# Issuing 16 small row-to-column DMAs from GpSimd's queue instead of ScalarE's

## The chip, the cores and the metric

The kernel runs on one core of a Trainium2 chip. The metric is the time of one execution on the device in microseconds; the time before is the median of three runs. Traces come from one more execution under the hardware profiler. Engines are written as in the profile: PE is TensorE (PEld its weight loads), DVE VectorE, ACT ScalarE, POOL GpSimd, SP the sync engine, whose queue issues most DMAs; a q behind a name (SPq, ACTq) is that engine's instruction queue, waiting or issuing.

## The reference

A decoder of two layers on 256 tokens of width 1024, conditioned by a vector c. From silu(c) a matrix product gives each layer six vectors (shift, scale and gate of the mixer and of the experts) and two more for the shared keys and values. Layer 0 is a short gated convolution, layer 1 a causal differential attention with 8 heads; each is followed by 16 routed experts (one group of four, two experts in it). Cut to what matters:

```python
def reference(x, c, mod_w, mod_b, ...):
    c_act = jax.nn.silu(c)
    for l in range(DEPTH):
        m = c_act @ mod_w[l] + mod_b[l]
        sh_a, sc_a, gt_a, sh_f, sc_f, gt_f = jnp.split(m, 6, axis=-1)
        if l == N_A:
            k1, k2, v = shared_kv(x, c, kv_mod_w, kv_mod_b, kv_norm_g, kv_w)
        h = modulate(rmsnorm(x, norm_mix_g[l]), sh_a, sc_a)     # h * (1 + scale) + shift
        y = short_conv_mixer(h, ...) if l < N_A else diff_attention(h, k1, k2, v, ...)
        x = x + gt_a[:, None, :] * y
        h = modulate(rmsnorm(x, norm_ffn_g[l]), sh_f, sc_f)
        y = hier_moe(h, ...)
        x = x + gt_f[:, None, :] * y
    return rmsnorm(x, final_norm_g)
```

## The kernel before

All weights, some 295 MB in float32, pass once through the core. They are cut into tiles of 1 MB (128 partitions of 8 KB) in one long list, `stream`, in the order of use; `upto` issues them one after the other on SP's queue (line 162) into a pool of 15 buffers, `w`. SP thus runs ahead of the computation until it must wait for a buffer to be read out.

The projections (conv in and out, key/value, query, output) split each weight into a high part `whi` (a copy to float32r, line 58, on ACT, a few of the output weights on GpSimd, line 198) and a low part `wlo` (a subtraction on VectorE, line 61), some three steps ahead of TensorE (lines 228 and 233). The experts use the weights as they are: line 599 multiplies by w1 and w3, line 627 by w2, 12 tiles for a pair of experts, eight pairs in each layer.

The conditioning vectors are made beside this by the class `Vecs`: eight `step`s, each with one 1 MB tile, put into the projection loops by `tick`, accumulate 2048 values in one PSUM bank (line 323). At the eighth step ACT copies them to SBUF as `vrow` (line 328): four rows of 512. Some of the vectors are wanted as columns, value d on partition d / 8, since modulation works by partition there. For these, `column` issues two DMAs of 2 KB each, 64 partitions of 8 values, from one row of `vrow` into a tile `pcs` (line 336). This happens in six of the seven vector groups: 2, 2, 4, 4, 2 and 2 DMAs. The columns are read by VectorE in `shift_scale` (lines 365 and 367). Each engine runs its instructions in the order in which the program is written (the schedule is manual); so in ACT's queue the DMAs stand right behind `vrow` and ahead of the next weight parts and PSUM copies.

How a DMA tells that it has landed is not written in the kernel but laid out by the tile framework: DMAs issued by SP and ACT share eight completion counters (DMAHW0 to DMAHW7 in the built program), which they take in turn, and those issued by GpSimd take eight others (DMASW0 to DMASW7). An issue waits until everything that was put on its counter before has landed.

Of the kernel before, what the change touches and what calls it, by code (L numbers as in the profile page):

```python
# [33 lines left out]
def tile_yoco_trunk(ctx: ExitStack, tc: tile.TileContext,  # L34
# [5 lines left out]
    PE, V, A, G = nc.tensor, nc.vector, nc.scalar, nc.gpsimd  # L40
# [266 lines left out]
    class Vecs:  # L307
# [24 lines left out]
        def column(self, v):  # L332

            c = self.cols[v] = sm.tile([128, K], F32, name="pcs", bufs=4)
            for h in range(2):
                A.dma_start(c[64 * h:64 * h + 64], self.rows[32 * (2 * v + h):32 * (2 * v + h) + 1])

        def columns(self):

# [616 lines left out]
    for j in range(4):  # L956
# [18 lines left out]
        for u in range(2):  # L975
            if j < 2:
                h = 4 * j + 2 * u
# [228 lines left out]
```

## Time and profile before

| | |
|---|---|
| median of three runs | 818.91 us (818.17 to 819.31) |
| the profiled execution | 820.68 us, its span 818.9 us |
| TensorE busy | 748.8 us, 91% of the span |
| ScalarE, VectorE, GpSimd busy | 221.2, 274.1 and 78.9 us |
| mean granted TensorE clock | 0.984 |
| DMA | 296.76 MB, mean 362 GB/s, up to 423 GB/s in a slice |
| column DMAs on ACT's queue | 16 of 2 KB |

The span is from the first to the last instruction; the 1.8 us around it belong to the execution's time. Stages by time: vectors of the first layer and conv to 164 us, routing and experts of layer 0 to 412, keys, values and queries to 500, attention and output to 577, routing and experts of layer 1 to the end. In timelines the number in brackets is the time that the engine stood idle before the row and the work that ended it.

### The profile page before, as it was taken

The numbers are of one execution on the slowest core, as the hardware profiler recorded it, in microseconds if no ns is written. First come the engines' busy times: TensorE is split into PE (matmuls) and PEld (weight loads), VectorE is DVE, ScalarE is ACT, GpSimd is POOL, SyncE is SP. The second block draws the span as 40 slices with busy tenths as digits, with TensorE's granted clock in tenths as the row PEclk, the third lists the DMA queues.
The fourth block names the chain that finished last, engine by engine and source line by source line (L and its number), as shares of the span: only waits on it lengthen the run. The fifth ranks groups of instructions, "written<-read, shape, count | busy, mean of one in ns | idle before, by whom it ended". The sixth has DMA issues, their size and how long they took to land. (4 is left out here: it accounts for less than half of the span.)

```text
span 818.9 us, 10570 instructions
## 1 busy us (share of the span) xinstructions
PE 748.8 (91%) x4130; PEld 414.1 (51%) x4139; DVE 274.1 (33%) x586; ACT 221.2 (27%) x484; POOL 78.9 (10%) x97
## 2 busy tenths in 40 slices
PE   2899999999998799998879999998899999999985
PEld 2488786654343443332368577766543335434331
DVE  0337346462102312211272353674622124112113
ACT  3343233333010120010152454763321112111102
POOL 1000000100111011001030000332001110111001
PEclk9999999999999999999999999998999999999998
DMA  9999895839999999999999999685089999999993
GB/s 370 403 402 406 335 405 222 347 128 423 421 421 421 422 419 420 422 421 421 412 412 403 404 396 344 218 290 177 1 327 401 421 421 421 421 421 421 422 396 138
DMA packets 57734, 296.76 MB, mean 362 GB/s; under 512 B 6403, under 2 KB 6692, under 8 KB 26958
## 3 DMA queue, kind: packets, MB, share of 16 engines
q1 hardware_dynamic: 56326, 295.90, 90.0%
q8 instruction: 34, 0.56, 0.3%
q10 hardware_dynamic: 1352, 0.12, 0.1%
q14 instruction: 22, 0.18, 0.1%
HBM read 294.92 MB, written 1.05 MB: 361 GB/s over the span
## 5 line engine op out<-in xcount | busy, mean ns | idle before, releaser
L599 PE MATMUL pw<-w,xg 128*64 128x512 f32 x1024 | 230.1, 594 | 11.5 <-DMA w<-in_exp_w_dram 10.0
L599 PEld LDWEIGHTS pw<-w,xg 128*64 128x64 f32 x1024 | 76.8, 137 | 153.3 <-issue 127.6
L627 PE MATMUL py<-w,hidT 128*64 128x512 f32 x512 | 119.0, 597 | 7.0 <-DMA w<-in_exp_w_dram 4.8
L61 DVE TENSOR_TENSOR wlo<-w,whi 128x512 fp32r<-128x512 f32 x128 | 84.6, 694 | 114.8 <-ACT whi L58 103.0
L58 ACT ACTIVATE whi<-w 128x512 fp32r<-128x512 f32 x122 | 71.3, 625 | 53.0 <-PE pci L228 26.1
L608 DVE TENSOR_TENSOR silu<-silu,pw 128x512 f32<-128x512 f32 x16 | 11.0, 688 | 215.3 <-PE pw L599 215.3
L627 PEld LDWEIGHTS py<-w,hidT 128*64 128x64 f32 x512 | 36.5, 137 | 80.3 <-issue 62.1
L61 POOL TENSOR_TENSOR yl<-y,yh 128x512 fp32r<-128x512 f32 x28 | 35.5, 1269 | 372.0 <-ACT yh L58 372.0
L633 DVE SCALAR_TENSOR_TENSOR y<-py,cs,row 128x512 f32<-128x512 f32 x32 | 24.0, 751 | 104.8 <-PE py L627 102.1
L323 PE MATMUL pg<-w,cact 128*32 128x512 f32 x448 | 57.2, 615 | 0.0
L58 ACT ACTIVATE yh<-y 128x512 fp32r<-128x512 f32 x28 | 17.6, 630 | 110.3 <-DVE y L633 110.3
L652 DVE TENSOR_TENSOR xs<-xs,psx 128x512 f32<-128x512 f32 x64 | 41.0, 682 | 13.2 <-PE psx L651 8.1
L616 ACT ACTIVATE hidT<-pht 128x512 f32<-128x512 f32 x16 | 9.6, 598 | 124.1 <-PE pht L614 112.8
L228 PE MATMUL pci<-hTh,whi 128*128 128x256 f32 x192 | 33.8, 300 | 1.3 <-ACT hTh L58 1.3
L228 PEld LDWEIGHTS pci<-hTh,whi 128*128 128x128 f32 x192 | 27.5, 196 | 8.5 <-ACT whi L58 3.8
L228 PE MATMUL pci<-hTl,whi 128*128 128x256 f32 x192 | 31.2, 285 | 0.0
L228 PE MATMUL pci<-hTh,wlo 128*128 128x256 f32 x192 | 31.2, 285 | 0.0
L607 ACT ACTIVATE silu<-pw 128x512 f32<-128x512 f32 x16 | 9.5, 596 | 74.7 <-PE pw L599 74.7
L228 PEld LDWEIGHTS pci<-hTl,whi 128*128 128x128 f32 x192 | 26.9, 194 | 0.0
L228 PEld LDWEIGHTS pci<-hTh,wlo 128*128 128x128 f32 x192 | 26.9, 194 | 0.0
L567 PE MATMUL pgx<-ohe,xh 128*128 128x512 f32 x64 | 21.4, 474 | 4.9 <-DVE ohe L556 4.9
L651 PE MATMUL psx<-yh,sct 128*128 128x512 f32 x56 | 24.6, 440 | 0.0
(239 smaller groups left out, 857.2 us busy)
## 6 DMA issues: line engine op xcount, KB each, us to landing
w<-in_exp_w_dram SPq DMA_DIRECT2D x184, 1024.0 KB, 19.8
w<-in_mod_w_dram SPq DMA_DIRECT2D x48, 1024.0 KB, 13.1
w<-in_conv_in_w_dram SPq DMA_DIRECT2D x12, 1024.0 KB
w<-in_kv_mod_w_dram SPq DMA_DIRECT2D x8, 1024.0 KB, 14.9
w<-in_kv_w_dram SPq DMA_DIRECT2D x8, 1024.0 KB, 19.8
w<-in_exp_w_dram SPq DMA_DIRECT2D x12, 512.0 KB, 10.1
w<-in_conv_out_w_dram SPq DMA_DIRECT2D x4, 1024.0 KB
w<-in_q_w_dram SPq DMA_DIRECT2D x4, 1024.0 KB, 16.1
```

The costliest lines, as they stand in the source:

```text
L58: A.activation(hi, a, AF.Copy)
L61: eng.tensor_tensor(lo, a, hi.bitcast(F32), op=ALU.subtract)
L228: PE.matmul(self.p[b // 2][:, 256 * (b % 2):256 * (b % 2) + 256], lhsT=w[:, 128 * b:128 * b + 128], rhs=x, start=False, stop=last and b % ...
L323: PE.matmul(self.p[32 * j:32 * j + 32], lhsT=cact[:, k:k + 1].to_broadcast([128, 32]), rhs=w[:, half(j)], start=False, stop=k == K - 1)
L567: PE.matmul(p, lhsT=x[:, tt, k::8], rhs=self.oh[:, tt].rearrange("p e s -> p (e s)"), start=i + tt == 0, stop=i + tt == 2)
L599: PE.matmul(p[64 * i:64 * i + 64], lhsT=xg[:, k, c:c + 64], rhs=W((nm, l, es[i]), k), start=k == 0, stop=k == K - 1)
L608: V.tensor_mul(s, s, pw3)
L616: A.activation(hT, p.rearrange("p (k s) -> p k s", k=4), AF.Copy)
L627: PE.matmul(py[h][64 * i:64 * i + 64], lhsT=hT[:, k, 64 * i:64 * i + 64], rhs=w, start=k == 0, stop=k == 3)
L633: V.scalar_tensor_tensor(y, py[h], cs[:, n % 2:n % 2 + 1], row[:, half(h)], op0=ALU.mult, op1=ALU.mult)
L651: PE.matmul(p, lhsT=sel, rhs=v, start=i == 0, stop=i == 1)
L652: V.tensor_add(xs[:, tt, half(h)], xs[:, tt, half(h)], p)
```

## The change

The two DMAs of `column` are issued on GpSimd's queue. Nothing else in the source is touched.

```diff
             c = self.cols[v] = sm.tile([128, K], F32, name="pcs", bufs=4)
             for h in range(2):
-                A.dma_start(c[64 * h:64 * h + 64], self.rows[32 * (2 * v + h):32 * (2 * v + h) + 1])
+                G.dma_start(c[64 * h:64 * h + 64], self.rows[32 * (2 * v + h):32 * (2 * v + h) + 1])
```

In the built program the instructions of TensorE, VectorE and SP keep their order; ACT loses the 16 DMAs and GpSimd has them. Three places follow.

On SP's queue, around 96 to 134 us, stand the weight tiles of the conv output, of the key/value vectors and then of the experts, with the counters that each issue waits for (PE and DVE are the waits for the buffer). Before:

```order
L162 DMA w_905<-in_conv_out_w_dram 128x4x512 [waits DMAHW4_49,PE_49]
L162 DMA w_939<-in_conv_out_w_dram 128x4x512 [waits DMAHW7_49,DVE_49]
L162 DMA w_983<-in_kv_mod_w_dram 128x2048 [waits DMAHW0_49,PE_49]
L162 DMA w_1024<-in_conv_out_w_dram 128x4x512 [waits DMAHW1_49,DVE_49]
L162 DMA w_1062<-in_kv_mod_w_dram 128x2048 [waits DMAHW2_49,DVE_49]
L162 DMA w_1096<-in_kv_mod_w_dram 128x2048 [waits DMAHW3_49,PE_49]
L162 DMA w_1134<-in_kv_mod_w_dram 128x2048 [waits DMAHW4_49,PE_49]
L162 DMA w_1146<-in_kv_mod_w_dram 128x2048 [waits DMAHW5_49,PE_49]
```

and now:

```order
L162 DMA w_905<-in_conv_out_w_dram 128x4x512 [waits DMAHW2_49,DVE_49]
L162 DMA w_939<-in_conv_out_w_dram 128x4x512 [waits DMAHW3_49,PE_49]
L162 DMA w_983<-in_kv_mod_w_dram 128x2048 [waits DMAHW4_49,PE_49]
L162 DMA w_1024<-in_conv_out_w_dram 128x4x512 [waits DMAHW5_49,DVE_49]
L162 DMA w_1062<-in_kv_mod_w_dram 128x2048 [waits DMAHW6_49,DVE_49]
L162 DMA w_1096<-in_kv_mod_w_dram 128x2048 [waits DMAHW7_49,PE_49]
L162 DMA w_1134<-in_kv_mod_w_dram 128x2048 [waits DMAHW0_49,PE_49]
L162 DMA w_1146<-in_kv_mod_w_dram 128x2048 [waits DMAHW1_49,PE_49]
```

Before, counters 5 and 6 are left out between w_905 and w_939: two column DMAs hold them, and w_1146 is the first tile to meet counter 5 again. Now the tiles take the counters without a gap.

On ACT's queue at the last vector group ahead of the experts (pcs are the columns), about 174 us. Before:

```order
L328 ACTIVATE vrow_1659<-pg_1370 128x512 [waits DMAHW6_49,DMAHW5_49,PE_49]
L336 DMA pcs_1661<-vrow_1659 64x1x8 [waits DMAHW3_49,Activation_49]
L336 DMA pcs_1661<-vrow_1659 64x1x8 [waits DMAHW4_49]
L336 DMA pcs_1664<-vrow_1659 64x1x8 [waits DMAHW6_49]
L336 DMA pcs_1664<-vrow_1659 64x1x8 [waits DMAHW7_49]
L424 ACTIVATE xg_1676<-pgx_1680,f0sh_1512,f0gs_1510 128x256 [waits DVE_49]
```

and now:

```order
L328 ACTIVATE vrow_1659<-pg_1370 128x512 [waits DMASW3_49,DMASW2_49,PE_49]
L424 ACTIVATE xg_1676<-pgx_1680,f0sh_1512,f0gs_1510 128x256 [waits DVE_49,Activation_49]
L424 ACTIVATE xg_1676<-pgx_1681,f0sh_1512,f0gs_1510 128x256 [waits DVE_49]
L424 ACTIVATE xg_1676<-pgx_1682,f0sh_1512,f0gs_1510 128x256 [waits DVE_49]
L424 ACTIVATE xg_1676<-pgx_1683,f0sh_1512,f0gs_1510 128x256 [waits DVE_49]
```

The four DMAs held counters 3, 4, 6 and 7, which the expert tiles of SP meet next; vrow now waits for GpSimd's counters, since the columns read the row before it.

On GpSimd's queue in the attention's seventh head (sms are a head's statistics, whi the high part of an output weight), about 549 us. Before:

```order
L1066 TENSOR_TENSOR sms_4167<-sms_4167,neghalf_110 128x2
L1067 TENSOR_TENSOR sms_4167<-sms_4167 128x2
L198 CAST whi_4361<-w_3815 128x512
L1066 TENSOR_TENSOR sms_4237<-sms_4237,neghalf_110 128x2
L1067 TENSOR_TENSOR sms_4237<-sms_4237 128x2
```

and now:

```order
L1066 TENSOR_TENSOR sms_4167<-sms_4167,neghalf_110 128x2
L1067 TENSOR_TENSOR sms_4167<-sms_4167 128x2
L336 DMA pcs_4330<-vrow_4328 64x1x8 x2
L198 CAST whi_4361<-w_3815 128x512
L1066 TENSOR_TENSOR sms_4237<-sms_4237,neghalf_110 128x2
L1067 TENSOR_TENSOR sms_4237<-sms_4237 128x2
```

The two column DMAs, and their wait for vrow, stand ahead of the cast.

## Rows read from the trace of the kernel before

**Rows 1.** The page's busy line: us (share of the span) xinstructions.
```profile
PE 748.8 (91%) x4130; PEld 414.1 (51%) x4139; DVE 274.1 (33%) x586; ACT 221.2 (27%) x484; POOL 78.9 (10%) x97
```

**Rows 2.** Timeline of DVE at two `shift_scale`: start, us, engine, line, tiles.
```profile
469.03 0.17 DVE L365 SCALAR_TENSOR_TENSOR a1gs<-pcs,Rc 128x8 f32<-128x8 f32 x1
...
563.02 0.17 DVE L365 SCALAR_TENSOR_TENSOR f1gs<-pcs,Rc 128x8 f32<-128x8 f32 x1
```

**Rows 3.** Waits of SP's queue, 110-140 and 150-180: total us, times, longest.
```profile
SPq L162 <- DMA pcs<-vrow: 18.2, 2, 17.9
...
SPq L162 <- DMA pcs<-vrow: 22.8, 2, 22.6
```

**Rows 4.** Two stretches: busy us by engine, granted clock, DMA share, GB/s.
```profile
125.00:135.00 10.00, 9.43 (x66) 7.62 (x65) 7.00 (x14) 2.89 (x6) 0.08 (x1) 1.00 0.10 30
160.00:176.00 16.00, 15.04 (x126) 8.80 (x126) 11.94 (x30) 4.83 (x8) 1.37 (x2) 1.00 0.02 5
```

**Rows 5.** Timeline of SP's queue and PE's vector steps, 160 to 191.
```profile
168.64 3.64 PE L323 MATMUL pg<-w,cact 128*32 128x512 f32 x32
...
176.24 8.37 SPq L162 DMA_DIRECT2D w<-in_exp_w_dram  x10
...
190.18 0.33 SPq L162 DMA_DIRECT2D w<-in_exp_w_dram  x1
```

**Rows 6.** PE's waits in 176 to 412, and PE's timeline at the last.
```profile
PE pw L599 <- DMA w<-in_exp_w_dram: 9.3, 8, 1.3
PE py L627 <- DMA w<-in_exp_w_dram: 3.8, 4, 1.1
...
401.85 1.08 PE L627 MATMUL py<-w,hidT 128*64 128x512 f32 x4 [1.07 <-DMA w<-in_exp_w_dram]
```

**Rows 7.** PE's waits in 588 to 812, the second expert layer.
```profile
PE py L627 <- DMA w<-in_exp_w_dram: 1.0, 1, 1.0
...
PE pw L599 <- DMA w<-in_exp_w_dram: 0.7, 1, 0.7
```

**Rows 8.** Line 336 as a group (ns min/median/max), and two batches in ACT's timeline.
```profile
L336 ACTq DMA_DIRECT2D pcs<-vrow x16: 471/606/865, 90.6 to 548.5; - x16
...
452.12 2.42 ACTq L336 DMA_DIRECT2D pcs<-vrow  x4
...
547.98 1.38 ACTq L336 DMA_DIRECT2D pcs<-vrow  x2
```

**Rows 9.** PE's timeline where it waits for ACT behind a batch.
```profile
135.07 0.74 PE L233 MATMUL po<-whi,hTh 128*128 128x512 f32 x2 [0.64 <-ACT whi L58]
...
456.24 0.74 PE L233 MATMUL pkv<-whi,hh 128*128 128x512 f32 x2 [1.87 <-ACT whi L58]
...
499.74 0.92 PE L1012 MATMUL psc<-kT,w 64*128 64x256 f32 x8 [0.56 <-ACT w L998]
...
550.34 0.59 PE L1077 MATMUL pot<-ident,on 128*128 128x128 f32 x2 [0.97 <-ACT on L1071]
```

**Rows 10.** POOL's timeline: its longest instruction.
```profile
123.44 1.64 POOL L61 TENSOR_TENSOR hTl<-yT,hTh 128x512 fp32r<-128x512 f32 x1 [1.58 <-ACT hTh L58]
```

**Rows 11.** DVE's timeline: the first use of head 1's bias.
```profile
506.92 0.42 DVE L1021 CUSTOM_DVE_ANT_0 w<-psc,bias 128x256 f32<-128x256 f32 x1
```

**Rows 12.** POOL and DVE around 549 to 553.
```profile
548.76 0.20 POOL L1067 TENSOR_TENSOR sms<-sms 128x2 f32<-128x2 f32 x1
548.89 0.61 POOL L198 CAST whi<-w 128x512 fp32r<-128x512 f32 x1
...
551.36 0.68 DVE L61 TENSOR_TENSOR wlo<-w,whi 128x512 fp32r<-128x512 f32 x1
...
552.70 0.18 DVE L1037 RECIPROCAL sms<-sms 128x4 f32<-128x4 f32 x1 [0.65 <-ACT w L1031]
```

**Rows 13.** DMA issues: queue, count, KB each, median us from issue to landing.
```profile
w<-in_exp_w_dram SPq DMA_DIRECT2D x184, 1024.0 KB, 19.8
...
pcs<-vrow ACTq DMA_DIRECT2D x16, 2.0 KB, 1.7
```

## The prediction

> **What bounds the kernel now.** I read the busy line of the page first: TensorE works 91% of the span, so a change pays only where TensorE stands still [rows 1]. The moved DMAs feed columns that are used 14 us and more after they are issued [rows 2], so their own landing holds nobody up. What they hold up is found in two other views.
>
> The first is the list of what the SP queue waits for. SP issues the whole weight stream in order. In 110 to 140 us its longest wait is for a column DMA, 17.9 us; in 150 to 180 us again, 22.6 us [rows 3]. This is odd, for no weight tile needs a column. The order of the built program says why: every DMA issued by SP or ACT takes one of eight completion counters in turn, and an issue waits until all that went on its counter before has landed. A column DMA sits on such a counter, but ACT issues it only when ACT gets there; SP, which runs ahead, meets it and stops, and all weights behind stop with it. Both show as silence on the DMA engines: share 0.10 in 125 to 135 and 0.02 in 160 to 176, so 9.0 + 15.7 us of stream time not used [rows 4]. When the second stop ends, at 176.24, SP issues ten tiles within 8.4 us; the next, the eleventh, waits for TensorE to free a buffer and goes out at 190.18 [rows 5].
>
> The second is what TensorE waits for. In the first expert layer (176 to 412) it waits 12 times for expert weights, 9.3 + 3.8 = 13.1 us, the last time at 401.85 [rows 6]. In the second layer, the same code with the stream full at its start, such waits come to 1.0 + 0.7 us [rows 7].
>
> **The change, part by part.** *Removed: 16 issues on ACT*, 471 to 865 ns each, median 606 [rows 8], 9.7 us in all. Most of it lies in ACT's idle time. On the path it lies where TensorE waits for an ACT instruction that stands right behind a batch. Those waits are 0.64 us at 135.07 (first weight parts of the conv output), 1.87 at 456.24 (behind a batch of 2.42 and the two kT copies), 0.56 at 499.74 (scores, behind qT) and 0.97 at 550.34 (head 6, behind a batch of 1.38) [rows 8, 9]. Each is smaller than its batch, so each can go whole: in the order, kT now stands directly behind vrow, and so in the other places. Together 4.04.
>
> *Moved: the completion counters.* GpSimd's DMAs count on eight counters of their own, so SP's counters now hold weight tiles alone and the stops fall away. What is late next is a free buffer, of which there are 15 of 1 MB. I size the gain at the second of them, the one that the expert layer inherits. A tile takes 1.0486 MB / 421 GB/s (the page's rate in the expert slices) = 2.49 us. Before, the eleventh tile behind the stop is served from 176.24 + 10 x 2.49 = 201.1. After, the ten earlier ones go out between 153 and some 181 us: eight take buffers that are read out by the vector steps ending at 172.3 (168.64 + 3.64) [rows 5] or before, two follow on the first expert's matmuls; at 2.49 each they are through by about 187 (an estimate from these rows). The eleventh still needs its buffer, which came free at 190.18, and 0.64 sooner now: 189.5. The head start is 201.1 - 189.5 = **11.6 us**. TensorE could use 13.1 + 0.64 = 13.7 by the end of that layer; the smaller counts, so 11.6, of which 0.64 is the first ACT term. Some 2.1 us of DMA waits stay, near the 1.7 of the second layer. The earlier stop gives nothing of its own: TensorE's waits name no DMA between 45 and 176.
>
> A rule of the Trainium skill speaks against this term: "DMA: Bandwidth & Descriptors", section "Issuing engines are not separate DMA queues", says that issuing from several engines only saves the sequencer's time of initiating. By it the sum would hold the 4.04 alone. The wait of 22.6 us on another queue's small DMA [rows 3] disagrees: the queues share counters here, and that is a matter of the program's bookkeeping, of which the rule doesn't speak.
>
> *After the first layer.* The stream stays 11.6 ahead, and TensorE names no DMA in 412 to 500, so 1.87 + 0.56 + 0.97 = 3.40 come on top: 15.0.
>
> *Added: 16 issues on GpSimd*, and a wait of GpSimd for vrow ahead of each batch. No row shows such an issue. Its price p per DMA is bounded by 0.47 us (the shortest on ACT) and 1.64 (GpSimd's longest working instruction [rows 10]); I take 1.1, the middle, since both ends are other kinds of work. There are six batches. Behind the first four stand on GpSimd: the low parts of the conv result, the residual add, the count for the overflow test, the bias of head 0, all needed far later than 4p. Behind the fifth, released at 497.9, stand the biases of heads 1 and 2; VectorE reads the first at 506.92 [rows 11], 8 us on, so it is covered. The sixth is not. At 548.76 GpSimd ends a head's scale, and the cast of an output weight (0.61) now stands behind two issues. VectorE takes that cast's result at 551.36 (0.68) ahead of RECIPROCAL of the next head, which would start 0.97 earlier than its 552.70 [rows 12]. Cast and subtraction end at 548.96 + 2p + 1.30; that passes 551.73 by 2p - 1.47: 0 at the low end, 0.7 at 1.1, 1.8 at 1.64.
>
> **Sum.** 15.0 - 0.7 = 14.3 us, off the profiled execution's own 820.68: 806.4. That execution stands 1.77 above the median of 818.91, so the median becomes **804.6**. Alone it spans 801.5 (stream fully repaid, p cheap: 13.7 + 3.4) to 807.
>
> **Rivals.**
> *Only ACT's issue time is saved.* SP's stops would be replaced by waits for buffers at the same places. For it: SP names buffers (TensorE, VectorE) for many waits in these stretches. Against it: ten tiles in 8.4 us after the stop, so the buffers had been free. Time: 818.91 - 4.04 + 0.7 = 815.6. Chance 0.08.
> *GpSimd's issue is dear.* VectorE is busy nearly throughout 549 to 552, and if the issue cannot proceed beside that work, the pair lasts until VectorE stops for want of the cast, about 552; cast, subtraction and RECIPROCAL then run late by some 2 to 4 us: 806 to 808.5. Chance 0.10. The Trainium skill, "SBUF — State Buffer", section "SBUF: two separate sides", says that a DMA from GpSimd cannot get its descriptors written while VectorE runs a two-port operation, 620 ns becoming 3100 ns. By that p the term would be 2 x 3.1 - 1.47 = 4.7 and the time 808.6; no run here shows it yet.
> *Slower: the columns land late.* VectorE takes its instructions in order, so a column that is missing at shift_scale (469.03, 563.02) stops the weight parts behind it [rows 2]. After the issues on GpSimd the cover is about 10.7 us at the fourth batch (452.1 + 4.4 to 467.2) and 10.9 at the last (551.2 to 562.1). A landing time L costs (L - 10.7) + (L - 10.9); it eats the 14.3 at L = 18, and at 20 the kernel is slower, 822. For it: a weight tile under a full stream takes 19.8 us to land. Against it: that tile stands behind seven others on its own queue, and a column DMA on ACT's queue landed in 1.7 [rows 13]. Chance 0.04.
> *Nothing measurable*, gains and losses cancelling: 0.03.
>
> **How the numbers follow.** Forecast 0.75, the rivals 0.08, 0.10, 0.04 and 0.03. Faster by over 0.2% (about what a measurement of this kernel can tell from no change) are the first three: 0.93; within it 0.03; slower 0.04. The range goes from 801.0 to 810.0: it takes in the forecast's ends and the dear issue, and leaves out the rest, some 0.17 with the tails.
>
> **What the profile after must show.** SP's waits name no column DMA; DMA share in 125 to 135 and 160 to 176 well over the 0.10 and 0.02 of before; TensorE's waits for expert weights in the first layer down from 13.1 to 1 to 3 us; the layer's last such wait some 11 to 12 us earlier; the 1.87 at the third value projection step gone; L336 on GpSimd's queue at about 1.1 us each, and DMA landing well under 10 us. The prediction is wrong if SP waits for buffers where it waited for columns, if the first layer stays short of weights, or if TensorE or VectorE now waits for a column or for GpSimd's cast.

## The result, and the profile after

The changed kernel takes 807.3 us (median of four runs, 806.41 to 807.42) where the kernel before, run beside it, takes 819.0: ratio 0.9856, 95% interval 0.9839 to 0.9873. Two further sets of runs give 807.29 against 819.51 (0.9849) and 807.17 against 820.7 (0.9843). So the gain is 11.7 to 13.5 us. The forecast was 804.6, range 801.0 to 810.0, a gain of 14.3: the time lies in the range, and the gain is 0.8 to 2.6 us smaller than forecast.

The page's busy line, us (share of the span) xinstructions, answers to [rows 1]: TensorE's work is the same within 0.5%, its share is 93% for 91%. GpSimd has 16 instructions more; the profile counts its DMA issues as work.

```profile
PE 745.3 (93%) x4139; PEld 413.3 (51%) x4139; DVE 274.3 (34%) x586; ACT 220.8 (27%) x484; POOL 87.7 (11%) x113
```

What SP's queue waits for in 110 to 140 and then in 150 to 180 us (total us, times, longest), the answers to [rows 3]:

```profile
SPq L162 <- PE pg L323: 17.4, 6, 6.3
SPq L162 <- DVE wlo L61: 8.8, 4, 3.3
...
SPq L162 <- PE pg L323: 16.7, 6, 7.6
SPq L162 <- DVE wlo L61: 12.7, 1, 12.7
```

No row names a column. What is left are waits for buffers that TensorE and VectorE still read, 26.2 and 29.4 us in all. That they are waits of another kind shows in the same two stretches that stand in [rows 4] (busy us by engine, granted clock, DMA share, GB/s):

```profile
125.00:135.00 10.00, 10.00 (x66) 8.26 (x65) 8.34 (x16) 4.81 (x10) 1.05 (x2) 1.00 1.01 420
160.00:176.00 16.00, 15.04 (x123) 9.05 (x122) 12.64 (x30) 4.83 (x8) 3.07 (x6) 1.00 0.71 254
```

30 GB/s became 420, and 5 became 254. TensorE's waits in 176 to 412, and then the last of them in its timeline, to be held against [rows 6]:

```profile
PE pw L599 <- DMA w<-in_exp_w_dram: 5.6, 5, 1.3
...
PE py L627 <- DMA w<-in_exp_w_dram: 2.1, 2, 1.1
```

```profile
390.16 1.08 PE L627 MATMUL py<-w,hidT 128*64 128x512 f32 x4 [1.05 <-DMA w<-in_exp_w_dram]
```

The last wait stands at 390.16 for 401.85, 11.7 us sooner; but 7.7 us of waits are left, not 1 to 3. Line 336 as a group (ns min/median/max, first and last start; its DMAs from issue to landing), for [rows 8] and [rows 13]:

```profile
L336 POOL DMA_DIRECT2D pcs<-vrow x16: 518/538/794, 89.9 to 535.5; - x16
...
DMA to landing us min/median/max: 4.8/5.2/6.6
```

### Where the time went, place by place

TensorE executes the same instructions in the same order in both kernels, so the start of one instruction in the two traces says how far the changed kernel is ahead there. TensorE's timeline of the kernel before and then of the changed kernel, at six such places (start, us, engine, line, tiles); two of the rows of before, 499.74 and 550.34, stand in [rows 9]:

```profile
83.63 0.76 PE L822 MATMUL prb<-R,ident 43*128 43x296 f32 x2
...
415.14 3.41 PE L411 MATMUL ph<-ident,xn 128*128 128x128 f32 x16 [4.29 <-DVE xn L403]
...
590.05 3.65 PE L599 MATMUL pw<-w,xg 128*64 128x512 f32 x16
...
809.00 1.98 PE L648 MATMUL psx<-y,sct 128*128 128x512 f32 x4 [0.88 <-DVE y L633]
```

```profile
82.62 0.76 PE L822 MATMUL prb<-R,ident 43*128 43x296 f32 x2
...
403.47 3.78 PE L411 MATMUL ph<-ident,xn 128*128 128x128 f32 x16 [4.31 <-DVE xn L403]
...
485.58 0.92 PE L1012 MATMUL psc<-kT,w 64*128 64x256 f32 x8
...
535.25 0.59 PE L1077 MATMUL pot<-ident,on 128*128 128x128 f32 x2
...
576.10 3.65 PE L599 MATMUL pw<-w,xg 128*64 128x512 f32 x16
...
794.86 1.98 PE L648 MATMUL psx<-y,sct 128*128 128x512 f32 x4 [0.88 <-DVE y L633]
```

One more pair comes from the group of the vector steps (line 323), whose first start in 395 to 560 is 425.8 before and 414.4 after.

| place | ahead, us | gained since the place above | in the sum |
|---|---|---|---|
| conv, ahead of any moved DMA (prb) | 1.01 | 1.01 | 0 |
| end of the first expert layer (ph) | 11.67 | 10.66 | 11.6 |
| first vector step of layer 1 | 11.4 | -0.27 | 0 |
| scores (psc), behind batches four and five | 14.16 | 2.76 | 1.87 + 0.56 = 2.43 |
| head 6 (pot), behind batch six | 15.09 | 0.93 | 0.97 - 0.7 |
| second expert layer (pw) | 13.95 | -1.14 | 0 |
| last scatter (psx) | 14.14 | 0.19 | 0 |
| end of the span, 818.9 and 805.2 | 13.7 | -0.44 | 0 |

The first 1.01 us has no term in the sum. It stands already at 43 us (the matmuls of line 319 that begin at 43.09 before and at 42.08 after), ahead of SP's first stop for a column, which begins after 77. It may still belong to the change, for it goes with the kernel: in the six traces of kernels that leave a small DMA on ScalarE's queue at the third batch, prb stands at 83.22 to 84.07, in the eight others at 81.76 to 82.85. How work at 174 us could bear on it no run shows.

Of the 10.66 us, 0.95 stand already at the first matmul of line 599 (178.69 before, 176.73 after; from prb 95.06 and 94.11), where ScalarE's first wait is gone, and 9.71 come in the expert layer.

The 1.14 us lost ahead of the second expert layer go with a longer spell of half clock, which the kernel before has too in its second trace. From the last pot of the attention to pw the first trace of before takes 28.96 us at a granted clock of 0.82 (561.09 to 590.05), its second trace 29.86 at 0.77, the traces of the changed kernel 29.84 to 30.07 at 0.77. Among all fourteen traces it is 29.84 to 30.07 at 0.77, 28.18 to 28.96 at 0.82 and 26.86 at 0.87. So the end of a single trace says less than its places.

### The profile page after: what moved, and what is told of

It reads as the page before. It is cut to its first block, busy times and chain, and to the rows that moved or that the text cites. A ratio compares the mean times of both kernels' runs of the same rounds, so it can differ in the third digit from the quotient of the medians.

```text
span 805.2 us, 10595 instructions
## 1 busy us (share of the span) xinstructions
PE 745.3 (93%) x4139; PEld 413.3 (51%) x4139; DVE 274.3 (34%) x586; ACT 220.8 (27%) x484; POOL 87.7 (11%) x113
## 5 line engine op out<-in xcount | busy, mean ns | idle before, releaser
L599 PEld LDWEIGHTS pw<-w,xg 128*64 128x64 f32 x1024 | 75.0, 137 | 149.9 <-issue 133.2
L627 PE MATMUL py<-w,hidT 128*64 128x512 f32 x512 | 117.3, 596 | 5.1 <-DMA w<-in_exp_w_dram 3.1
```

Of the source, the lines that this page charges most:

```text
L599: PE.matmul(p[64 * i:64 * i + 64], lhsT=xg[:, k, c:c + 64], rhs=W((nm, l, es[i]), k), start=k == 0, stop=k == K - 1)
L627: PE.matmul(py[h][64 * i:64 * i + 64], lhsT=hT[:, k, 64 * i:64 * i + 64], rhs=w, start=k == 0, stop=k == 3)
```

## Experiments

All kernels below differ from the kernel before or from the changed one in the lines shown. In the traces of all of them the place ph less the place prb says how long TensorE took from the conv to the end of the first expert layer, free of the start; "layer" below is that time less the changed kernel's 403.47 - 82.62 = 320.85. The kernel before has 415.14 - 83.63 = 331.51, so its layer is +10.66. In its second trace it is +10.33, and in two more traces of the changed kernel +0.07 and +0.70: a layer repeats within some 0.7 us.

### The kernel before, once more

> The kernel before, unchanged, profiled once more, to see which parts of one profiled execution repeat. If the first execution was slow by a start of its own (TensorE was 1.0 us later by 48 us than in the changed kernel, before any moved DMA), this one has a span of about 817 us, and SP's waits for column DMAs again come to about 59 us, 22.6 us of it in 150 to 180. If it repeats at 818.9, the 1.0 us belongs to the kernel.

The span was 818.8 us, the one time 820.53, and 17 runs of the kernel before in that set have a median of 820.14. The prb row stands at 83.44, so the later start repeats. SP's wait in 110 to 190 us:

```profile
SPq L162 <- DMA pcs<-vrow: 44.0, 5, 22.6
```

SP's wait repeats to the tenth, and the expectation of 817 was wrong: the profiled execution of before (820.68) was typical. In sets of 11 to 17 runs its median is 819.5 to 820.8; the first three, 818.91, were on the low side.

### Only the third batch on GpSimd

```diff
-                G.dma_start(c[64 * h:64 * h + 64], self.rows[32 * (2 * v + h):32 * (2 * v + h) + 1])
+                (G if self.key[1] == "kvm" else A).dma_start(c[64 * h:64 * h + 64], self.rows[32 * (2 * v + h):32 * (2 * v + h) + 1])
```

> Only the third batch of columns (four DMAs, about 174 us, the last ahead of the experts) is issued by GpSimd, the other five stay on ScalarE. Theory of the counters: the wait of 22.6 us on SP's queue goes, and with it some 10.7 us of the first expert layer; the waits of TensorE behind ScalarE's other batches stay (4.4 us): 808 to 810.5 us. Theory of ScalarE's issue time: TensorE waits for nothing behind the third batch, so no gain: 819.0, within 0.5.

811.16 us against 820.14, ratio 0.9893 (0.9869 to 0.9917): 9.0 us gained by moving four DMAs, though TensorE waits for nothing of ScalarE's right behind them. The time is above the expected 808 to 810.5, which was counted from 819.0; the gain is within the expected 8.5 to 11. Layer +1.10, of which 0.95 is ScalarE's first wait, still there. ScalarE's issue time as the cause of the whole gain is refuted by this run alone. The wait behind the fourth batch is there as before (TensorE's timeline, as in [rows 9]):

```profile
446.58 0.73 PE L233 MATMUL pkv<-whi,hh 128*128 128x512 f32 x2 [1.87 <-ACT whi L58]
```

### Only batches four to six on GpSimd

```diff
-                G.dma_start(c[64 * h:64 * h + 64], self.rows[32 * (2 * v + h):32 * (2 * v + h) + 1])
+                (G if self.key[1:3] == ("mod", 1) else A).dma_start(c[64 * h:64 * h + 64], self.rows[32 * (2 * v + h):32 * (2 * v + h) + 1])
```

> Only the fourth to sixth batch (452 to 548 us) are issued by GpSimd, the first three stay on ScalarE. Theory of the counters: just the three waits of TensorE behind ScalarE go, 1.87 + 0.56 + 0.97 = 3.4 us: 815.6, between 815 and 816.8. Theory of ScalarE's issue time: these three waits are most of the whole gain of 11.7: about 809 to 811.

816.67 against 820.14, ratio 0.9958 (0.9945 to 0.9972): 3.5 us, the 3.4 of the three waits. Layer +10.16, as before. The two halves, 9.0 and 3.5, make 12.5, which is the whole gain of 11.7 to 13.5.

### The third batch undone

```diff
-                G.dma_start(c[64 * h:64 * h + 64], self.rows[32 * (2 * v + h):32 * (2 * v + h) + 1])
+                (G if self.key[1] != "kvm" else A).dma_start(c[64 * h:64 * h + 64], self.rows[32 * (2 * v + h):32 * (2 * v + h) + 1])
```

> The changed kernel with one part undone: the third batch (four DMAs, about 174 us) is on ScalarE again, the other twelve stay on GpSimd. Theory of the counters: the four hold four counters, SP's list stops at its 69th DMA until about 175, as in the kernel before, and the whole gain of the layer, 9 to 10.7 us, is lost: 9 to 10.7 above the changed kernel (about 815 to 817); SP's one wait for a column is 20 to 23 us. Theory of ScalarE's issue time: nobody waits behind these four, so within 0.5 of the changed kernel.

816.07 beside the changed kernel's 807.29 in the same set: 8.8 us lost, a little under the lower bound of 9. Layer +9.88. SP's wait in 150 to 180 us is back:

```profile
SPq L162 <- DMA pcs<-vrow: 23.2, 3, 22.7
```

The changed kernel, run in that set for comparison:

> The changed kernel once more, on the same chip and beside the same runs as the three that follow, since single executions differ by 1 to 2 us in the short spells of half clock. Expected: 11 to 12.5 us under the kernel before; in the trace SP's waits name no column DMA, and TensorE at 412 us is 10 to 11 us ahead of the kernel before, start apart.

It came as expected, 12.2 us under the kernel before, with ph - prb 321.1 us against 320.9 in its first trace.

### The counters by dose

If a small DMA on ScalarE's queue hurts because it holds a counter, then a DMA that nobody needs must hurt as much. One such DMA, and then eight, behind the vrow of the third batch; all columns stay on GpSimd. The larger dose is shown; the smaller has one such line and a tile of K columns:

```diff
                 for v in self.want:
                     self.column(v)
+                if self.key[1] == "kvm":
+                    d = sm.tile([128, 8 * K], F32, name="dup", bufs=1)
+                    for i in range(8):
+                        A.dma_start(d[0:64, K * i:K * i + K], self.rows[0:1])
```

> The changed kernel, and one more DMA of 2 KB on ScalarE's queue, behind the vrow of the third batch, into a tile that nobody reads; all columns stay on GpSimd. Theory of the counters: this one DMA holds one of the eight counters; the stream stops at the eighth DMA after it in program order, tile 72 of SP's list, which went out at 167.79 and will go out at about 175 (in the kernel before four such DMAs stopped the fifth, tile 69). Seven tiles of 2.49 us from 174.8 end at 192.2, 4.0 later than the eleventh tile's issue at 188.2; the layer loses 3 to 4 us: 810.3 to 811.3 us. Theory of ScalarE's issue time: at most the 0.6 us of one issue: 807.3 to 807.9.

> The changed kernel and eight more DMAs of 2 KB on ScalarE's queue behind the vrow of the third batch, each into a place of its own in a tile that nobody reads. One such DMA stopped SP's list at its 72nd DMA and cost the layer 2.2 us in the trace, four (the columns themselves) stopped it at the 69th and cost 9.8. Eight hold all counters: by the built program the 66th DMA, which went out at 137, waits for the second of them, until about 175.4. Thirteen tiles of 2.49 us from there end at 207.8, 19.6 behind the 188.2 of the changed kernel; less the 1 to 3 us by which the two smaller doses fell short of this sum: 16.5 to 18.5 us, 823 to 827 us, slower than the kernel before. Theory of ScalarE's issue time: 4.8 us of issues end at 177.3, where the next work of ScalarE stood at 176.0: at most 1.5 us, 807 to 809.

SP's waits in 150 to 180 us with one DMA, then with eight:

```profile
SPq L162 <- DMA dup<-vrow: 11.4, 1, 11.4
```

```profile
SPq L162 <- DMA dup<-vrow: 40.9, 1, 40.9
```

The 72nd DMA of SP's list in SP's timeline, in the changed kernel and with one:

```profile
167.79 0.33 SPq L162 DMA_DIRECT2D w<-in_exp_w_dram  x1
```

```profile
174.93 0.33 SPq L162 DMA_DIRECT2D w<-in_exp_w_dram  x1
```

The places in SP's list count all its DMAs.

| small DMAs on ScalarE at 174 us | first DMA of SP's list that stops | SP's longest wait | layer, us | time |
|---|---|---|---|---|
| none (changed kernel) | - | - | 0 | 807.2 to 807.3 |
| one, unused | 72nd | 11.4 | +2.15 | 808.83 |
| four, the columns (third batch undone) | 69th | 22.7 | +9.88 | 816.07 |
| eight, unused | 66th | 40.9 | +18.45 | 825.65 |

The stop moves forward in the stream with the number of counters held, as the built program has it, and the layer's loss follows: 16 KB that nobody reads cost some 18 us (18.45 in the layer, 18.4 by the times of different sets, some 17 by their ratios) and make the kernel slower than the one before (ratio 1.0055, 1.0041 to 1.0070). For eight the expectation was 823 to 827. For one it was 3 to 4 us; the place of the stop and its end at 174.93 were right, the loss was 2.15 in the layer and some 1.6 in the time. That time alone cannot be told from the changed kernel's (ratio 0.9865, 0.9842 to 0.9888, for 0.9849 and 0.9843 in other sets), so for one DMA the loss rests on the trace. Its shortfall is the same error as in the prediction's sum, below: the stream's delay is counted at one tile, and part of it is absorbed later. Start apart, SP is 3.4 us behind the changed kernel at its 120th DMA (280.92 for 276.88) and 2.3 at its 123rd (295.83 for 292.92).

### ScalarE's time given back, the counters free

```diff
                 for v in self.want:
                     self.column(v)
+                    for _ in range(3):
+                        fill = sm.tile([128, 216], BF16, name="fill", bufs=1)
+                        A.activation(fill, self.rows[:, 0:216], AF.Copy)
```

> The changed kernel, but behind each vrow ScalarE makes three copies of 128x216 into a scratch tile for each pair of columns, in place of the two DMAs that left it: ScalarE's time is given back, the counters stay free. Theory of the counters: the layer's gain stays, and the 3.4 to 4.4 us of TensorE's waits behind ScalarE come back: 3.4 to 4.4 above the changed kernel (810.5 to 812), no wait of SP for a small DMA. Theory of ScalarE's issue time: all is lost, as in the kernel before, 819 to 820.

812.56 beside 807.29 in the same set, 5.3 us lost; the ratio to the kernel before, 0.992 (0.9897 to 0.9944), keeps the other 7 us. The copies took 9.2 us for the 9.7 of the removed issues. The copies as a group (busy us, mean ns | idle before them), and the waits that are back in TensorE's timeline, as in [rows 9]:

```profile
L333 ACT ACTIVATE fill<-vrow 128x216 bf16<-128x216 f32 x24 | 9.2, 384 | 0.8
```

```profile
446.83 0.73 PE L233 MATMUL pkv<-whi,hh 128*128 128x512 f32 x2 [1.76 <-ACT whi L58]
...
490.23 0.92 PE L1015 MATMUL psc<-kT,w 64*128 64x256 f32 x8 [0.48 <-ACT w L1001]
```

SP names no small DMA, the layer is at +1.73. The loss of 5.3 is above the expected 3.4 to 4.4: 0.91 of it shows at ScalarE's first wait (95.02 from prb to pw), 3.65 from the layer's end to head 6 (135.43 for 131.78), the rest is not placed. So the two effects stand apart: counters about 9, ScalarE's time 3.5 to 5.

### Every issue on GpSimd made twice

```diff
                 G.dma_start(c[64 * h:64 * h + 64], self.rows[32 * (2 * v + h):32 * (2 * v + h) + 1])
+                d = sm.tile([128, K], F32, name="dup", bufs=4)
+                G.dma_start(d[64 * h:64 * h + 64], self.rows[32 * (2 * v + h):32 * (2 * v + h) + 1])
```

> The changed kernel with every column DMA made twice on GpSimd, the second into a scratch tile: 32 issues of about 0.54 us. This measures what an issue on GpSimd costs where its cover ends. By the formula of the sum, two issues at the sixth batch cost 2 x 0.58 - 1.47 = nothing, four cost 4 x 0.58 - 1.47 = 0.85 us; the other places stay covered: 0.5 to 1.2 above the changed kernel. If the issue were dear there (blocked while VectorE works), 2 to 4 us. If it is hidden by something that the formula misses, nothing.

807.56 beside 807.29: no difference that the times can tell, where 0.5 to 1.2 was expected. The 32 issues take 0.52 to 0.79 us each. VectorE at the sixth batch, in the changed kernel and with doubled issues (idle time and its end in brackets):

```profile
536.64 0.69 DVE L61 TENSOR_TENSOR wlo<-w,whi 128x512 fp32r<-128x512 f32 x1 [0.27 <-POOL whi L198]
537.62 0.18 DVE L1037 RECIPROCAL sms<-sms 128x4 f32<-128x4 f32 x1 [0.29 <-ACT w L1031]
```

```profile
538.69 0.69 DVE L61 TENSOR_TENSOR wlo<-w,whi 128x512 fp32r<-128x512 f32 x1 [1.57 <-POOL whi L198]
539.30 0.17 DVE L1039 RECIPROCAL sms<-sms 128x4 f32<-128x4 f32 x1
```

With two issues RECIPROCAL still waits for ScalarE, not for the cast, so the issues cost nothing. With four, VectorE waits 1.57 us for the cast and RECIPROCAL starts right behind its subtraction: the cover is gone, as the formula of the sum says. TensorE pays at the next head, which needs what follows RECIPROCAL. Its timeline at head 6 and at the head behind it, in the changed kernel (its row at head 6, 535.25, stands above) and then with doubled issues:

```profile
540.48 0.59 PE L1077 MATMUL pot<-ident,on 128*128 128x128 f32 x2 [0.86 <-ACT on L1071]
```

```profile
536.01 0.59 PE L1079 MATMUL pot<-ident,on 128*128 128x128 f32 x2
...
542.22 0.59 PE L1079 MATMUL pot<-ident,on 128*128 128x128 f32 x2 [1.31 <-ACT on L1073]
```

At head 6 it is 0.76 us behind the changed kernel (0.23 of it stood at prb), at the next 1.74: the price is 0.98, where 0.85 was expected. In this trace the stretch ahead of the second expert layer, at a granted clock of 0.82 instead of 0.77, gives 1.13 of it back, and in the median of six runs 1 us is hardly more than the spread; so the time alone misses a price that the place shows.

### The first two batches back on ScalarE

```diff
-                G.dma_start(c[64 * h:64 * h + 64], self.rows[32 * (2 * v + h):32 * (2 * v + h) + 1])
+                (G if self.key[1:3] != ("mod", 0) else A).dma_start(c[64 * h:64 * h + 64], self.rows[32 * (2 * v + h):32 * (2 * v + h) + 1])
```

> The changed kernel with the first two batches (90 and 132 us) back on ScalarE, the other twelve DMAs on GpSimd. SP's waits for columns of 14 to 18 us at 78 to 93 and 116 to 134 come back, but TensorE waits for no weights before the expert layer, and the stream has its buffers full again by 172: only the 0.6 to 1.0 us of TensorE's wait behind the second batch, 808 to 808.5. If these earlier stops are worth stream time too, 4 us or more: above 811.

> The kernel with the first two batches back on ScalarE again, now beside the changed kernel on the same chip, since it came out at 806.47, 0.9828 of the kernel before, where the changed kernel had 0.9849 and 0.9856 in other sets of runs. The trace of the first try showed a loss of 0.96 us at the second batch, as the sum has it, and later gains where TensorE's clock was at half for a shorter time. If the trace's place is right, it is 0.5 to 1 us slower than the changed kernel in a set of its own; if the difference of the sets was real, 1.5 to 2 us faster.

> The changed kernel, beside the run above on the same chip: 11.5 to 12.5 us under the kernel before, as in its two other sets.

The first set gave 806.47 (0.9828, 0.9812 to 0.9843), faster than the expected 808 to 808.5. Beside the changed kernel in one set it is 807.47 against 807.17: the same within what the runs can tell (0.5 to 1 slower was expected), and the faster look of the first set did not repeat. SP's waits for the first two batches, in 60 to 190 us of the first trace, are back, 33.2 us of them:

```profile
SPq L162 <- DMA pcs<-vrow: 33.2, 3, 17.9
```

TensorE waits for no weights behind these stops. What TensorE does lose is ScalarE's first wait: from prb to pw both traces take 95.1 us, as the kernel before, for the changed kernel's 94.1. The layer is +2.18 in the first trace and +0.94 in the second, whose set has the changed kernel at +0.70. None of the kernels tried is shown to beat the changed one.

## Why the prediction was right, and where it was off

**The stops of SP's queue were the mechanism, and the third batch was the one that counted: right.** The silence on the DMA engines ended, SP names no column, and the one batch moved alone gains 9.0 us, undone alone loses 8.8. The rival in which buffers take the place of the columns falls. The prediction named as a sign of being wrong that SP waits for buffers where it waited for columns; SP does so now, but with 420 and 254 GB/s moved in the stretches that had 30 and 5. The sign was put badly, since a stream that has filled its buffers waits too.

**The size of the head start: 11.6 in the sum, 10.66 measured.** Of the 11.6, the sum gave 0.64 to ScalarE's first wait and 10.96 to the stream; TensorE gained 0.95 and 9.71. The eleventh tile went out at 188.21, 1.97 before its 190.18, as the sum had it but for the 1.01 of the start and 0.3 more of ScalarE's wait. Later tiles were as far ahead as the sum says, then lost some. SP's timeline, three issues of the kernel before and the same three of the changed one, behind the eleventh tile's:

```profile
289.81 0.33 SPq L162 DMA_DIRECT2D w<-in_exp_w_dram  x1
295.42 0.33 SPq L162 DMA_DIRECT2D w<-in_exp_w_dram  x1
304.95 0.34 SPq L162 DMA_DIRECT2D w<-in_exp_w_dram  x1
```

```profile
188.21 0.33 SPq L162 DMA_DIRECT2D w<-in_exp_w_dram  x1
...
276.88 0.33 SPq L162 DMA_DIRECT2D w<-in_exp_w_dram  x1
284.83 0.33 SPq L162 DMA_DIRECT2D w<-in_exp_w_dram  x1
292.92 0.34 SPq L162 DMA_DIRECT2D w<-in_exp_w_dram  x1
```

The stream is 12.93 ahead at 277 (11.9 without the start), 10.59 at the next tile, 12.03 after. In between SP waits for a buffer that the second matmul of an expert reads: 5.5 us in 268 to 296, against 3.2 us in 280 to 308 of the kernel before.

```profile
SPq L162 <- PE py L627: 5.5, 1, 5.5
```

```profile
SPq L162 <- PE py L627: 3.2, 1, 3.2
```

A stream that is further ahead meets full buffers earlier, and 0.9 us of the head start (12.93 to 12.03) ended there. The step that failed is "the smaller counts": it took the head start at 190 us as kept until the layer's end and looked for no second place with full buffers. Why buffers are short just there was not tried.

**What TensorE could use: 13.7 in the sum, more in truth.** In the expert layer 9.71 us were gained, while the listed waits for weights fell by 5.4 (13.1 to 7.7): 4.3 us came from beyond the list. One part is that the list gives the idle time and not the loss. TensorE's timeline has, for the same sixty-four matmuls of line 599, before and after the change:

```profile
256.73 0.59 PE L599 MATMUL pw<-w,xg 128*64 128x512 f32 x1
...
262.45 3.65 PE L599 MATMUL pw<-w,xg 128*64 128x512 f32 x16 [1.27 <-DMA w<-in_exp_w_dram]
267.42 3.65 PE L599 MATMUL pw<-w,xg 128*64 128x512 f32 x16 [1.32 <-DMA w<-in_exp_w_dram]
272.38 3.65 PE L599 MATMUL pw<-w,xg 128*64 128x512 f32 x14 [1.30 <-DMA w<-in_exp_w_dram]
275.96 0.50 PE L651 MATMUL psx<-yh,sct 128*128 128x512 f32 x1
```

```profile
252.93 13.90 PE L599 MATMUL pw<-w,xg 128*64 128x512 f32 x64
266.76 0.50 PE L651 MATMUL psx<-yh,sct 128*128 128x512 f32 x1
```

From the first to the product behind them they take 19.23 us with three stops and 13.83 without: three listed waits of 3.9 us together cost 5.4. The other part is TensorE at half clock (1.2 of 2.4 GHz) for a moment in that layer, before the change and not after it, some 1.6 us by an estimate from the clock of these 40 us; the last three columns are the granted clock, the DMA share and GB/s:

```profile
260.00:300.00 40.00, 34.21 (x146) 18.30 (x145) 9.95 (x17) 7.29 (x15) 3.21 (x3) 0.96 1.02 422
```

```profile
260.00:300.00 40.00, 38.03 (x176) 20.26 (x174) 9.89 (x17) 7.81 (x16) 2.54 (x2) 1.00 1.01 420
```

Some 1 us is not accounted for by these rows. So "some 2.1 us of DMA waits stay" and the sign "1 to 3 us" were wrong; the number did not enter the sum, since the head start was the smaller of the two.

**ScalarE's waits: right.** 2.43 expected behind batches four and five, 2.76 measured; 0.97 behind the sixth, 0.93 measured; moved alone they gave 3.5 us for 3.40. The 0.64 at 135 us, which the sum put inside the head start, was 0.95: the seven traces with DMAs or copies on ScalarE at the second batch take 95.02 to 95.08 us from prb to pw, the seven others 94.09 to 94.14. In the time it can't be seen: with the first two batches undone that is the same within 0.3 us, and these runs don't resolve 1 us.

**GpSimd's price: half of what was taken.** 0.538 us at the median, where the bounds were 0.47 and 1.64 and 1.1 was taken. With 0.58 (two in 1.16 us at the sixth batch) 2p - 1.47 is below zero: the 0.7 of the sum is nothing, the low end of its range. The formula itself held: with doubled issues it gives 0.85, and 0.98 was measured.

**The dear issue: refuted here.** At the third batch GpSimd's issues took 523 to 562 ns while VectorE worked beside all but the end of the last, the longest anywhere 794. The line of VectorE's timeline that stands beside the four issues of 172.8 to 174.9 us:

```profile
172.54 2.07 DVE L395 SCALAR_TENSOR_TENSOR xl<-xs,rstd,xh 128x512 fp32r<-128x512 f32 x3
```

The Trainium skill, "SBUF — State Buffer", section "SBUF: two separate sides", speaks of a GpSimd DMA of 620 ns that takes 3100 when it overlaps a copy by VectorE. The prediction put that for the issue; no issue here came near 3100 ns. The runs don't show whether a VectorE operation of that kind would do it.

**Late columns: refuted.** A landing takes 5.2 us where ScalarE's took 1.7 [rows 13]; the cover was 10.7.

**The Trainium skill's rule** that issuing from several engines only saves the sequencer's time of initiating ("DMA: Bandwidth & Descriptors", section "Issuing engines are not separate DMA queues") would have left 815.6. The dose runs show what it leaves out: eight unused 2 KB DMAs on another engine's queue held the weight stream for 40.9 us.

**From the sum to the median: the larger error, and some luck.** The sum gave 806.4 for the profiled execution, and the profiled execution took 807.22, 0.8 more: too much by 0.9 at the head start, too little by 1.0 at ScalarE's and GpSimd's terms together, and the rest in parts that have no term: 1.01 us of gain that stood at prb, 1.14 of loss in the spell of half clock ahead of the second expert layer, and small ones. That these cancel so far is luck. The step that failed most was the 1.77 us taken off to come from that execution to the median of three runs. The changed kernel's profiled executions (807.20 to 807.29) stand at its medians, and those of the kernel before (820.68 and 820.53) near its own, once 11 to 17 runs are taken. Without that step the forecast would have been 806.4 against 807.2 to 807.3. (Two side sums are slightly off and bear on nothing: 13.7 + 3.4 off 818.91 is 801.8, not 801.5, and a landing of 20 us would give some 823, not 822.)

## What to carry to other kernels

Read the waits of the queue that feeds the weights by name: a wait for a tile that its DMA does not use is bookkeeping, here a completion counter shared with another engine's queue, and a 2 KB transfer that is issued late can hold back megabytes. Count such stops where the consumer later runs short, not where they stand: the earlier stops of 15 to 18 us cost nothing that these runs could tell, the last one 9 to 10. Take a head start along the whole stretch to its use, since the next place with full buffers takes a part of it. And look for a small price at its place in the trace: a spell of half clock further on can hide 1 us in the time.

## What the runs showed that was not expected

A column DMA issued by GpSimd lands 5.2 us after its issue, one issued by ScalarE 1.7; the issue itself is shorter on GpSimd (0.538 against 0.606 us). And executions of programs that are the same instruction by instruction up to 174 us differ at prb (82.62 and 82.38 in two traces of the changed kernel, 83.49 with the third batch undone), by as much as the smaller terms of the sum; the granted clock in 20 to 50 us is 0.94 in the kernel before and 0.89 in the changed one, with TensorE ahead in the second. These starts go with the kernel, as said above. What sets them was not settled.
